# Expert layer: 224 tokens instead of 256 fetch their experts, in full 128-row gathers, and 288 instead of 256 meet all experts

## The chip, the cores and the metric

The kernel runs on one core of one Trainium2 chip. The metric is the device time of one execution in microseconds (us). A core has TensorE (PE; its weight loads are PEld), VectorE (DVE), ScalarE (ACT), GpSimd (POOL) and SyncE (SP), and 16 DMA engines that serve the queues of SP, ACT and POOL. MB are 10^6 bytes here, KB are 1024 bytes.

## The reference, cut to what matters

The program is two transformer blocks over 512 tokens of width 1024. The change is in the expert layer of the first block, where every token chooses 128 of 16384 experts (8 heads, 16 each) by two rounds of top-16 over products of keys:

```
s_top, i_top = lax.top_k(scores, PEER_TOPK)            # scores against 2 x 128 sub-keys per head
cand     = s_top[..., 0, :, None] + s_top[..., 1, None, :]
best, pos = lax.top_k(cand.reshape(..., 256), PEER_TOPK)
idx   = i_top[0] * 128 + i_top[1]   (at pos)           # 128 experts of each token
gates = jax.nn.softmax(best, axis=-1)
u = expert_u[it]; v = expert_v[it]                     # rows of 1024 fp32, 4 KB each
act = jax.nn.gelu(jnp.einsum("td,ted->te", xt, u), approximate=False)
return jnp.einsum("te,ted->td", gt * act, v)
```

## The kernel before

`peer()` computes this sum in two ways at once, for two halves of the tokens.

**The fetching tokens** (`NT = 256`, two tiles of 128 tokens, one token to a partition). For slot s of a tile, an indirect DMA from POOL (`fetch`, L1034) brings one expert row of 4 KB to each of the 128 partitions: 512 KB. `product` (L1005 in the profile, where the helper `dve` records everything) then multiplies it on DVE with the token's input row (`xt`) and sums it, for table `er`, or adds it with its gate to the output `y`, for table `ev`. That is 2 tiles x 128 slots x 2 tables = 512 gathers and 512 products. The rows lie in a ring of 8 in the buffers `xh` and `xl`; gathers are issued 6 products ahead (`LEAD`).

**The meeting tokens** (`ND = 256`) meet all 16384 experts in dense matmuls, 128 experts ("a row") at a time. In steps 0 to 127 of the loop `hidden(r)` multiplies 512 KB of weights of row r with the tokens `xb` (8 matmuls in fp32, which the trace shows as 16 records, L1078), and ACT applies the gelu a step later (L1085). In steps 128 to 255 `value(i)` multiplies row `order_v[i]` of the second table with gelu times gate (L1336), eight sums at once. The results of the gelu go to DRAM in pairs of rows (`ge_d`, L1089) and come back in the value steps (`ge`, L1301); the last `KEEP` = 16 rows stay. The gates stand in a grid `G` of 128 x 128 experts per token: `spread` builds it with one-hot matmuls, four tokens to a grid step (L1272 on PE; `sq` on DVE; `acc`, `gs` on ACT), writes it to DRAM 16 tokens at a time (L1278), and it is read back 16 rows at a time (L1316).

**The order.** The loop in `experts` writes the order of every engine by hand, step by step. `ROW` says how much DVE time by a planning rule a step takes (hidden rows without and with a grid step, value rows); `PACE` how far apart in such time two products stand, before and after the end of the top-16 work; `self.known` how many slots' indices exist. The top-16 work of `select` runs on DVE for tile 0, then for the two tiles of meeting tokens (2 and 3), then for tile 1: until that last one has made its `ix`, only the 128 slots of tile 0 can be gathered for table `er`, and the products stand one to a step or a little more. After it they stand about three to a step. In this text the **select stretch** goes from the first hidden matmul to the last reduction of `select`, the **gather stretch** from there to the landing of the last gather, and the **value stage** is the part of it with the value matmuls.

SP loads the weights in nine buffers in turn (`wraw`, `whi`, `wlo`, three each), so up to nine rows ahead of PE. Behind the loop the `y` tiles are transposed on PE (L1389) and added to `h`.

Of the kernel before, what the change touches and what calls it, by code (L numbers as in the profile page):

```python
# [18 lines left out]
T = 512  # L19
# [117 lines left out]
NT = 256  # L137
# [18 lines left out]
class Build:  # L156
# [809 lines left out]

    def peer(self):
        tc = self.tc
        with tc.tile_pool(name="pg", bufs=1) as pg:
# [12 lines left out]
            self.xt = pg.tile([128, 2, D], F32, name="xt")  # L982
# [44 lines left out]

    def fetch(self, upto):

        while self.nr < upto:  # L1030
            table, n = divmod(self.nr, 256)
            tt, s = divmod(n, 128)
            m = TOK[tt]
            self.nc.gpsimd.indirect_dma_start(  # L1034
                out=self.row(self.nr)[:m], out_offset=None,
                in_=self.A[("er", "ev")[table]].rearrange("j p a b -> (j p) (a b)"),
                in_offset=bass.IndirectOffsetOnAxis(ap=self.ix[:m, tt, s:s + 1], axis=0))
            self.nr += 1

    def product(self, pace):  # L1040

        n = self.nf
        if n >= self.known or self.spent < self.when + pace:
            return False
        self.when = self.spent
        self.fetch(n + 1)
        table, n = divmod(n, 256)
        tt, s = divmod(n, 128)
        m = TOK[tt]
        r = self.row(self.nf)[:m]  # L1050
        self.nf += 1
        if table == 0:
            self.dve("scalar_tensor_tensor", r, r, 1.0, self.xt[:m, tt], op0=OP.mult,
                     op1=OP.mult, accum_out=self.hid[:m, tt, s:s + 1])
        else:
            a, y = self.gate[:m, tt, s:s + 1], self.y[tt][:m]
# [6 lines left out]
        if table == 0 and s == 127:  # L1063
            h = self.hid[:m, tt]
            self.nc.scalar.activation(h, h, AF.Gelu)

            def weighted():
                self.dve("tensor_tensor", self.gate[:m, tt], self.gate[:m, tt], h, op=OP.mult)
            self.later(1, weighted)
        return True  # L1070
# [21 lines left out]
    def experts(self, pt, pw, pps):  # L1092
# [11 lines left out]
        self.gs2 = pw.tile([128, 2, 2048], F32, name="gs")  # L1104
        self.idx = pw.tile([128, 2, 5, 128], F32, name="idx")
# [35 lines left out]
        def select(tt, h0, n):  # L1141
# [88 lines left out]
            v("tensor_tensor", gt, gt, sm[:, :, None].to_broadcast([128, n, K]), op=OP.mult)  # L1230
            if TOK[tt] < 128:
                def turn():
                    tp = pps.tile([128, 4, 128], F32, name="gp", bufs=3)
                    idx = idx2[tt] = self.idx[:, tt % 2]
                    for i, t in enumerate((fin[:, 0], fin[:, 1], gt)):
                        te.transpose(tp[:, i], fl(t), self.ident)
                    s.activation(idx[:, :3], tp[:, :3], AF.Copy)
                    for i in range(2):
                        s.activation(idx[:, 3 + i], tp[:, 1 - i], AF.Copy, scale=-1.0)
# [3 lines left out]
        def spread(tt):  # L1243
# [6 lines left out]
            for tb in range((128 - TOK[tt]) // 16):  # L1250
                gs = gs2[:, tb % 2].rearrange("p (i t) -> p i t", t=16)
                for t4 in range(4):
                    o1 = self.nq.tile([128, 4, 128], F32, name="sq")
                    o2 = self.nq.tile([128, 4, 128], F32, name="acc")
                    i0 = TOK[tt] + tb * 16 + t4 * 4
# [30 lines left out]
        grids = (x for tt in (2, 3) for x in spread(tt))  # L1286
# [4 lines left out]
        order_v = [*range(119, 111, -1), *range(127, 119, -1), *range(111, -1, -1)]  # L1291
# [12 lines left out]
        def gates(i):  # L1304
# [3 lines left out]
            if i == 0:  # L1308
                self.gt2 = [pt.tile([128, NB * 256], F32, name="q")]
                self.y = [pt.tile([128, D], F32, name="kz"), pw.tile([128, D], F32, name="eq")]  # L1310
                self.a = pw.tile([128, 1280], F32, name="idx")
# [26 lines left out]
        with self.tc.manual_schedule(engines=ENGINES):  # L1338
            for r in range(5):
                load(r)  # L1340
            for tt in range(2):
                for half in range(2):
# [5 lines left out]
                    s.activation(self.xt[:m, tt, half * 512:(half + 1) * 512], tp[:m], AF.Copy)  # L1348
            end = 0.0
            while self.step < 256:  # L1350
# [15 lines left out]
                while self.spent < end:  # L1366
                    if self.product(PACE[work is None]):
                        continue
                    if work is None:
                        self.spent = end if self.nf == 512 else min(end, self.when + PACE[1])  # L1370
                    elif next(work, "end") == "end":
                        work = None
# [6 lines left out]
            assert not self.after  # L1379
        self.xh, self.xl = (self.cp.tile([128, 8, T], F32R, name=n) for n in ("xh", "xl"))  # L1380
        for d in range(8):
            h = self.h[:, d, NT:]
            v("tensor_tensor", h, h, yb[d][:, :ND], op=OP.add)
        for d in range(0, 8, 2):
            tp = self.pp.tile([128, T], F32, name="mm").rearrange("p (e t) -> p e t", e=2)
            for e in range(2):
                for tt in range(2):
                    m = TOK[tt]
# [634 lines left out]
```

## Time and profile before

| | before |
|---|---|
| median of 3 runs | 2758.99 us (2758.08 to 2763.65) |
| the profiled execution's own time | 2758.39 us |
| its span, first to last instruction | 2756.6 us |
| PE / PEld / DVE / ACT / POOL busy | 2442.9 / 2014.3 / 1831.3 / 932.0 / 1318.0 us |
| mean granted TensorE clock | 0.961 |
| DMA | 601.29 MB, mean 218 GB/s |

The busy times are sums over the whole program, in which stages with different limits follow each other. The expert layer's loop is the stretch from 615.6 us to 1833 us. A DMA share over 1 means that packets of the 16 engines overlap in the records.

### The profile page before, as it was taken

How to read it: one execution, taken by the hardware profiler on the slowest of the kernel's cores; microseconds unless marked ns; L12 is line 12 of the kernel's file. 1: busy time of each engine (PE TensorE's matmuls, PEld its weight loads, DVE VectorE, ACT ScalarE, POOL GpSimd, SP SyncE). 2: the span in 40 equal slices, each digit the busy share in tenths (PEclk: the TensorE clock that was granted, in tenths of full speed). 3: DMA queues.
4: the chain of work that ended last, by engine and by line, in shares of the span. 5: the costliest groups of instructions: out<-in, count | busy, mean ns of one | idle time of the engine just before them, and what ended most of it. 6: DMA issues, size and time to landing. Idle time of an engine off the chain costs nothing.

```text
span 2756.6 us, 33222 instructions
## 1 busy us (share of the span) xinstructions
PE 2442.9 (89%) x11548; PEld 2014.3 (73%) x11548; DVE 1831.3 (66%) x3674; ACT 932.0 (34%) x1806; POOL 1318.0 (48%) x930
## 2 busy tenths in 40 slices
PE   7999998999999999757777777888999998999997
PEld 5778877878889888646566666666777786777776
DVE  6655353367999997576676666785697758666226
ACT  4433243331148887000000000023477634333323
POOL 5433357343333235366566555654324555545543
PEclk9999999999999999979999899999999999999998
DMA  5311123139999999999999999952202352222332
GB/s 194 102 59 31 47 80 123 47 126 336 350 338 346 344 346 413 413 406 410 409 409 408 408 409 408 407 206 66 77 24 74 95 161 88 85 92 85 105 115 86
DMA packets 195368, 601.29 MB, mean 218 GB/s; under 512 B 23808, under 2 KB 44928, under 8 KB 193792
## 3 DMA queue, kind: packets, MB, share of 16 engines
q1 hardware_dynamic: 101664, 299.28, 31.1%
q0 software_dynamic: 73728, 268.47, 25.1%
q10 hardware_dynamic: 19808, 31.42, 3.2%
q8 instruction: 92, 1.51, 0.2%
q14 instruction: 76, 0.62, 0.1%
HBM read 556.62 MB, written 42.47 MB: 217 GB/s over the span
## 4 chain that ended last, share of the span: by engine, by line
PE 31%; DVE 27%; DMA 23%; issue 8%; ACT 6%; POOL 5%; ACTq 0%; DVEq 0%; POOLq 0%; SPq 0%
DMA xl<-in_ev_dram,ix 8%; DMA xl<-in_er_dram,ix 8%; DMA xh<-in_ev_dram,ix 7%; PE mm L227 7%; PE mm L228 6%; PE mm L226 6%; DVE y L1907 5%; PE mm L1078 3%; DVE xl L1005 2%; ACT whi L219 2%; DVE xh L1005 2%; PE dl L740 2%; DVE sq L1005 1%; POOL xh L1034 1%; POOL wlo L222 1%
## 5 line engine op out<-in xcount | busy, mean ns | idle before, releaser
L222 POOL TENSOR_TENSOR wlo<-wraw,whi 128x1024 fp32r<-128x1024 f32 (+5 forms) x212 | 466.0, 2203 | 463.0 <-ACT whi L219 458.2
L219 ACT ACTIVATE whi<-wraw 128x1024 fp32r<-128x1024 f32 (+4 forms) x213 | 204.3, 965 | 780.2 <-DMA wraw<-in_w_in_dram 517.5
L228 PE MATMUL mm<-xh,wlo 128*128 128x512 f32 (+1 forms) x1016 | 407.6, 402 | 18.6 <-POOL wlo L222 18.6
L227 PE MATMUL mm<-xl,whi 128*128 128x512 f32 (+1 forms) x1016 | 407.2, 401 | 5.9 <-DVE xl L341 3.1
L226 PE MATMUL mm<-xh,whi 128*128 128x512 f32 (+1 forms) x1016 | 402.9, 400 | 7.8 <-ACT xh L338 3.7
L1034 POOL DMA_INDIRECT xh<-in_er_dram,ix x128 | 149.6, 1169 | 214.2 <-DVE xh L1005 78.4
L228 PEld LDWEIGHTS mm<-xh,wlo 128*128 128x128 f32 (+1 forms) x1016 | 192.7, 190 | 65.8 <-POOL wlo L222 29.9
L227 PEld LDWEIGHTS mm<-xl,whi 128*128 128x128 f32 (+1 forms) x1016 | 192.9, 190 | 49.4 <-DVE xl L341 8.6
L1034 POOL DMA_INDIRECT xl<-in_er_dram,ix x128 | 137.2, 1072 | 191.1 <-DVE xl L1005 63.7
L226 PEld LDWEIGHTS mm<-xh,whi 128*128 128x128 f32 (+1 forms) x1016 | 192.7, 190 | 46.8 <-ACT xh L338 4.1
L1034 POOL DMA_INDIRECT xl<-in_ev_dram,ix x128 | 155.7, 1216 | 112.3 <-DVE eq L1005 38.5
L1034 POOL DMA_INDIRECT xh<-in_ev_dram,ix x128 | 151.4, 1183 | 100.9 <-DVE kz L1005 39.0
L1005 DVE SCALAR_TENSOR_TENSOR xh<-xh,xt 128x1024 f32<-128x1024 f32 x128 | 156.0, 1218 | 54.9 <-DMA xh<-in_er_dram,ix 54.5
L1907 DVE SCALAR_TENSOR_TENSOR y<-u,cvec,y 128x511 f32<-128x511 f32 (+1 forms) x88 | 137.3, 1563 | 74.3 <-ACT y L1905 72.8
L1005 DVE SCALAR_TENSOR_TENSOR xl<-xl,xt 128x1024 f32<-128x1024 f32 x128 | 155.9, 1218 | 41.7 <-DMA xl<-in_er_dram,ix 41.2
L1078 PE MATMUL mm<-xb,wlo 128*128 128x256 f32 x672 | 154.7, 384 | 8.7 <-DMA wlo<-in_eu_dram 8.7
L1078 PE MATMUL mm<-xb,whi 128*128 128x256 f32 x688 | 155.6, 379 | 2.6 <-DMA whi<-in_eu_dram 2.6
L1078 PE MATMUL mm<-xb,wraw 128*128 128x256 f32 x688 | 155.6, 379 | 0.0
L1078 PEld LDWEIGHTS mm<-xb,wlo 128*128 128x128 f32 x672 | 127.9, 193 | 26.5 <-issue 9.4
L1078 PEld LDWEIGHTS mm<-xb,whi 128*128 128x128 f32 x688 | 129.1, 190 | 19.6 <-issue 3.0
L1078 PEld LDWEIGHTS mm<-xb,wraw 128*128 128x128 f32 x688 | 129.1, 190 | 16.7
L1085 ACT ACTIVATE ge<-mm 128x256 f32<-128x256 f32 x128 | 48.4, 378 | 230.3 <-PE mm L1078 229.6
(671 smaller groups left out, 5371.1 us busy)
## 6 DMA issues: line engine op xcount, KB each, us to landing
wraw<-in_w_in_dram SPq DMA_DIRECT2D x57, 512.0 KB, 3.5
wraw<-in_w_up_dram SPq DMA_DIRECT2D x44, 512.0 KB, 3.5
wraw<-in_eu_dram SPq DMA_DIRECT2D x43, 512.0 KB, 6.9
whi<-in_eu_dram SPq DMA_DIRECT2D x43, 512.0 KB, 6.9
wlo<-in_ev_dram SPq DMA_DIRECT2D x43, 512.0 KB, 7.0
wraw<-in_ev_dram SPq DMA_DIRECT2D x43, 512.0 KB, 7.2
wlo<-in_eu_dram SPq DMA_DIRECT2D x42, 512.0 KB, 7.0
whi<-in_ev_dram SPq DMA_DIRECT2D x42, 512.0 KB, 7.2
```

The source lines that it names most:

```text
L219: nc.scalar.activation(hi, src, AF.Copy)
L222: (eng_lo or nc.vector).tensor_tensor(lo, src, hi.bitcast(F32), op=OP.subtract)
L226: t.matmul(ps, wh, xh, start=first, stop=False)
L227: t.matmul(ps, wh, xl, start=False, stop=False)
L228: t.matmul(ps, wl, xh, start=False, stop=last)
L740: te.matmul(ps[:, h * 128:(h + 1) * 128], lhs(h), rhs(h), start=True, stop=True)
L1005: return getattr(self.nc.vector, name)(out, *a, **kw)
L1034: self.nc.gpsimd.indirect_dma_start(out=self.row(self.nr)[:m], out_offset=None, in_=self.A[("er", "ev")[table]].rearrange("j p a b -> (j p ...
L1078: nc.tensor.matmul(ps[:, :ND], w[:, k], self.xb[:, k], start=k == 0, stop=k == 7)
L1085: nc.scalar.activation(self.pair[:, r % 2], ps[:, :ND], AF.Gelu)
L1907: v.scalar_tensor_tensor(y[:, j:], u[:, :T - j], w(2 - j), y[:, j:], op0=OP.mult, op1=OP.add)
```

## The change

`NT` becomes 224 and `ND` 288. Tile 0 keeps 128 tokens. Tile 1 has 96 tokens; its slots 96 to 127 are spread over the partitions 96 to 127, which serve tokens 0 to 31 of the tile in slots 0 to 31, tokens 32 to 63 in slots 32 to 63, and tokens 64 to 95 in slots 64 to 95. So tile 1 needs 96 gathers for each table, of 128 rows each: 448 gathers and products in all. For that, `ix` and `gate` of tile 1 are patched by three small DMAs each from ACT, `xt` by three DMAs (two at the start, one after slot 31), and the part of `y` on the last 32 partitions is put aside in `ys` after slots 31 and 63. The transposes behind the loop become plain matmuls with the identity or a selecting matrix, four instead of two per 128 columns.

The dense side gets 288 columns: matmuls of 288 instead of 256, `ge` pairs of 288 KB, a `G` with 18 instead of 16 blocks of tokens, 72 instead of 64 grid steps. `KEEP` falls from 16 to 6, so 61 instead of 56 pairs go through DRAM. `ROW` and `PACE` get new numbers, with a third pace of 2.2 for the products in the value steps.

```diff
-NT = 256
+NT = 224
 ND = T - NT
 NB = ND // 16
-KEEP = 16
-PACE = (2.6, 1.4)
-ROW = (4.0, 4.65, 3.85)
+KEEP = 6
+PACE = (2.6, 1.4, 2.2)
+ROW = (4.15, 5.05, 3.95)
+SLOTS = 128 + 96
...
             self.nc.gpsimd.indirect_dma_start(
-                out=self.row(self.nr)[:m], out_offset=None,
+                out=self.row(self.nr), out_offset=None,
...
-            self.dve("scalar_tensor_tensor", r, r, 1.0, self.xt[:m, tt], op0=OP.mult,
-                     op1=OP.mult, accum_out=self.hid[:m, tt, s:s + 1])
+            c = tt and 1 + s // 32 % 2
+            self.dve("scalar_tensor_tensor", r, r, 1.0, self.xt[:, c], op0=OP.mult,
+                     op1=OP.mult, accum_out=self.hid[:, tt, s:s + 1])
+            if tt and s == 31:
+                self.nc.scalar.dma_start(self.xt[96:, 1], self.xt[64:96, 1])
...
+            if tt and s in (31, 63):
+                if s == 31:
+                    self.ys = self.pg.tile([128, 3, D], F32, name="xt")
+                    self.nc.gpsimd.memset(self.ys[:96, :2], 0.0)
+                self.dve("tensor_copy", self.ys[96:, s // 32], y[96:])
+                self.dve("memset", y[96:], 0.0)
...
-                v("tensor_copy", self.ix[:, tt, sl], fl(far))
-                self.known = 128 * tt + (h0 + n) * K if tt == 0 else 512
+                m = TOK[tt]
+                v("tensor_copy", self.ix[:m, tt, sl], fl(far)[:m])
+                if tt:
+                    for k in range(3):
+                        p = slice(32 * k, 32 * k + 32)
+                        nc.scalar.dma_start(self.ix[96:, 1, p], self.ix[p, 1, 96:])
+                self.known = 2 * SLOTS if tt else (h0 + n) * K
...
+            if tt == 1:
+                s.activation(self.gate[:96, 1], fl(gt)[:96], AF.Copy)
+                for k in range(3):
+                    p = slice(32 * k, 32 * k + 32)
+                    nc.scalar.dma_start(self.gate[96:, 1, p], self.gate[p, 1, 96:])
...
-        grids = (x for tt in (2, 3) for x in spread(tt))
+        grids = (x for tt in (2, 3, 1) for x in spread(tt))
...
-                    if self.product(PACE[work is None]):
+                    if self.product(PACE[2 if i >= 0 else work is None]):
...
-                    te.transpose(tp[:, e, tt * 128:tt * 128 + m],
-                                 self.y[tt][:m, (d + e) * 128:(d + e + 1) * 128],
-                                 self.ident[:m, :m])
+                te.matmul(tp[:, e, :128], self.y[0][:, c], self.ident, start=e == 0, stop=False,
+                          skip_group_check=True)
+                te.matmul(tp[:, e, 128:NT], self.y[1][:, c], sel, start=False, stop=False,
+                          skip_group_check=True)
+                for k in range(2):
+                    o = 128 + 32 * k
+                    te.matmul(tp[:, e, o:o + 32], self.ys[:, k, c], self.ident[:, 96:],
+                              start=False, stop=k == 1, skip_group_check=True)
```

Where the end of the top-16 work falls can be read on ACT. The store `ge_d_43NN` is that of the hidden rows 2NN and 2NN+1, and the load of the exponential's table (L1225 before, L1244 after) stands at the end of tile 1's `select`. Before:

```order
L1085 ACTIVATE ge<-mm 128x256
L1089 DMA ge_d_4346<-ge 128x512
...
L1085 ACTIVATE ge<-mm 128x256
L1275 ACTIVATE gs<-gp 128x4x128
L1257 ACTIVATE acc<-row,idx 128x128 x4
L1258 ACTIVATE acc<-acc 128x512
L1225 ACT_TABLE_LOAD
L1225 ACTIVATE gate<-gate 128x128
```

and after the change, with the six small DMAs that patch `ix` and `gate`:

```order
L1098 ACTIVATE ge<-mm 128x288
L1102 DMA ge_d_4343<-ge 128x576
...
L1098 ACTIVATE ge<-mm 128x288
...
L1236 DMA ix<-ix 32x32 x3
L1244 ACT_TABLE_LOAD
L1244 ACTIVATE gt__7768<-gt__7768 128x128
L1251 ACTIVATE gate<-gt__7768 96x128
L1254 DMA gate<-gate 32x32 x3
```

The end of the top-16 work moved six hidden rows forward, from behind the gelu of row 94 to behind that of row 88. On DVE, 115 products (the rows that write `hid`) stand ahead of tile 1's cast to `ix` in both orders, and 148 rows `sq<-row,idx` before, 132 after.

In the value steps, DVE's order shows how many products (`kz<-xl,gate,kz`) stand to a value row (`idx<-ge,gs`, which makes the row's right-hand side). Before:

```order
L1005 TENSOR_TENSOR idx<-ge,gs 128x256
L1005 SCALAR_TENSOR_TENSOR kz<-xl,gate,kz 128x1024
L1005 SCALAR_TENSOR_TENSOR kz<-xh,gate,kz 128x1024
L1005 SCALAR_TENSOR_TENSOR kz<-xl,gate,kz 128x1024
L1005 TENSOR_TENSOR idx<-ge,gs 128x256
L1005 SCALAR_TENSOR_TENSOR kz<-xh,gate,kz 128x1024
L1005 SCALAR_TENSOR_TENSOR kz<-xl,gate,kz 128x1024
L1005 TENSOR_TENSOR idx<-ge,gs 128x256
```

and after:

```order
L1008 TENSOR_TENSOR idx<-ge,gs 128x288
L1008 SCALAR_TENSOR_TENSOR kz<-xh,gate,kz 128x1024
L1008 SCALAR_TENSOR_TENSOR kz<-xl,gate,kz 128x1024
L1008 TENSOR_TENSOR idx<-ge,gs 128x288
L1008 SCALAR_TENSOR_TENSOR kz<-xh,gate,kz 128x1024
L1008 TENSOR_TENSOR idx<-ge,gs 128x288
```

Before, two or three products stand to a value row, after it one or two. Over all, 205 products of 512 stand ahead of the first value row's turn in the loop before, and 230 of 448 after.

## Rows read from the trace of the kernel before

**Rows 1.** The span in 40 equal slices: DMA share, GB/s.

```profile
DMA  5311123139999999999999999952202352222332
GB/s 194 102 59 31 47 80 123 47 126 336 350 338 346 344 346 413 413 406 410 409 409 408 408 409 408 407 206 66 77 24 74 95 161 88 85 92 85 105 115 86
```

**Rows 2.** Stretches: length, busy (x instructions), granted clock, DMA share, GB/s.

```profile
615.60:1019.70 404.10, 389.33 (x1985) 345.71 (x1984) 368.22 (x1195) 213.35 (x504) 134.02 (x122) 1.00 0.96 342
1019.70:1196.50 176.80, 131.35 (x643) 113.09 (x641) 116.40 (x223) 67.67 (x162) 82.15 (x82) 0.90 1.02 405
1196.50:1833.10 636.60, 501.12 (x2049) 407.47 (x2050) 445.48 (x509) 3.21 (x4) 385.79 (x313) 0.93 1.01 400
1019.70:1821.20 801.50, 621.41 (x2641) 511.21 (x2640) 554.59 (x720) 69.04 (x164) 461.87 (x391) 0.92 1.02 405
```

**Rows 3.** The chain that ended last: start, length, what, around 1020 us.

```profile
1017.42 2.20 DVE fin L1005
...
1029.04 10.26 DMA xl<-in_er_dram,ix
```

**Rows 4.** Gathers (L1034) in the two stretches: POOL busy, clock, DMA share, GB/s.

```profile
615.60:1019.70 404.10, 134.02 (x122) 1.00 0.96 342
1019.70:1821.20 801.50, 459.92 (x390) 0.92 1.02 405
```

**Rows 5.** DMA issues, whole span: count, KB each, median us to landing.

```profile
G<-gs SPq DMA_DIRECT2D x16, 1024.0 KB, 10.8
...
ge<-ge_d SPq DMA_DIRECT2D x56, 256.0 KB, 7.5
...
q<-G SPq DMA_DIRECT2D x4, 2048.0 KB, 11.4
```

**Rows 6.** DMA issues from 615.6 to 1019.7 us.

```profile
ge_d<-ge ACTq DMA_DIRECT2D x47, 256.0 KB, 6.6
G<-gs SPq DMA_DIRECT2D x11, 1024.0 KB, 9.7
```

**Rows 7.** PE in order of time: start, length; hidden rows without, then with grid steps.

```profile
674.90 3.62 PE L1078 MATMUL mm<-xb,wraw 128*128 128x256 f32 x16
678.36 3.62 PE L1078 MATMUL mm<-xb,whi 128*128 128x256 f32 x16
...
866.83 1.05 PE L1272 MATMUL gp<-acc,sq 128*128 128x128 f32 x8
867.72 2.54 PE L1078 MATMUL mm<-xb,wlo 128*128 128x256 f32 x11
```

**Rows 8.** L1078 in the select stretch: PE and PEld busy (x records), clock, DMA.

```profile
615.60:1019.70 404.10, 340.96 (x1537) 288.62 (x1538) 1.00 0.96 342
```

**Rows 9.** L1272 in the select stretch, the same columns.

```profile
615.60:1019.70 404.10, 50.45 (x384) 50.42 (x384) 1.00 0.96 342
```

**Rows 10.** Waits from 1300 to 1800 us: us in total, times, longest.

```profile
PEld sp L1336 <- DVE idx L1005: 140.6, 71, 7.4
...
DVE kz L1005 <- DMA xh<-in_ev_dram,ix: 41.0, 43, 4.4
```

**Rows 11.** PE in order of time, at value row 49, behind a load of G.

```profile
1440.51 1.35 PEld L1336 LDWEIGHTS sp<-idx,wraw 128*128 128x128 f32 x4 [7.18 <-DVE idx L1005]
...
1442.38 2.34 PE L1336 MATMUL gp<-idx,wraw 128*128 128x256 f32 x6
```

**Rows 12.** Behind the loop, in order of time: the transposes and the sums after them.

```profile
1833.09 0.27 PE L1389 MATMUL mm<-ident,kz 128*128 128x128 f32 x1
...
1834.86 0.27 PE L1389 MATMUL mm<-ident,eq 128*128 128x128 f32 x1
...
1839.68 1.47 POOL L307 TENSOR_TENSOR acc<-acc,sq 128x512 f32<-128x512 f32 x1 [0.83 <-ACT sq L303]
...
1841.98 1.47 POOL L307 TENSOR_TENSOR acc<-acc,sq 128x512 f32<-128x512 f32 x1 [0.83 <-ACT sq L303]
```

**Rows 13.** Products on DVE, gather stretch: busy, mean ns; idle before.

```profile
L1005 DVE SCALAR_TENSOR_TENSOR kz<-xh,gate,kz 128x1024 f32<-128x1024 f32 x63 | 81.0, 1285 | 41.1 <-DMA xh<-in_ev_dram,ix 40.0
```

More of the change, by code (lines that the diff above doesn't have):

```diff
@@ L981, in peer @@
             self.xb = pg.tile([128, 8, ND], F32, name="xb")
-            self.xt = pg.tile([128, 2, D], F32, name="xt")
+            self.xt = pg.tile([128, 3, D], F32, name="xt")
             self.ix = pg.tile([128, 2, 128], U32, name="ix")
@@ L1046, in product @@
         self.fetch(n + 1)
[L1047 to L1050, printed above, removed]
+        table, tt, s = self.slot(n)
+        r = self.row(n)
         self.nf += 1
         if table == 0:
-            self.dve("scalar_tensor_tensor", r, r, 1.0, self.xt[:m, tt], op0=OP.mult,
-                     op1=OP.mult, accum_out=self.hid[:m, tt, s:s + 1])
+            c = tt and 1 + s // 32 % 2
[3 more added lines that the diff above has]
+                self.nc.scalar.dma_start(self.xt[96:, 1], self.xt[64:96, 1])
         else:
-            a, y = self.gate[:m, tt, s:s + 1], self.y[tt][:m]
+            a, y = self.gate[:, tt, s:s + 1], self.y[tt]
             if s == 0:
@@ L1060, in product @@
                 self.dve("scalar_tensor_tensor", y, r, a, y, op0=OP.mult, op1=OP.add)
+            if tt and s in (31, 63):
[4 more added lines that the diff above has]
+                self.dve("memset", y[96:], 0.0)
         self.spent += 0.08
         self.fetch(min(self.nf + LEAD, self.known))
-        if table == 0 and s == 127:
-            h = self.hid[:m, tt]
+        n = 96 if tt else 128
+        if table == 0 and s == n - 1:
+            h, g = self.hid[:, tt, :n], self.gate[:, tt, :n]
             self.nc.scalar.activation(h, h, AF.Gelu)
-            def weighted():
-                self.dve("tensor_tensor", self.gate[:m, tt], self.gate[:m, tt], h, op=OP.mult)
-            self.later(1, weighted)
+            self.later(1, lambda: self.dve("tensor_tensor", g, g, h, op=OP.mult))
         return True
@@ L1103, in experts @@
                allow_small_or_imprecise_dtypes=True)
-        self.gs2 = pw.tile([128, 2, 2048], F32, name="gs")
-        self.idx = pw.tile([128, 2, 5, 128], F32, name="idx")
+        self.gs2 = pw.tile([128, 2, NB * 128], F32, name="gs")[:, :, :2048]
+        self.idx = pw.tile([128, 5 * ND], F32, name="idx")
         qq = pt.tile([128, 2, NB * 128], F32, name="q")
@@ L1310, in gates @@
                 self.y = [pt.tile([128, D], F32, name="kz"), pw.tile([128, D], F32, name="eq")]
-                self.a = pw.tile([128, 1280], F32, name="idx")
+                self.a = pw.tile([128, 5 * ND], F32, name="idx")
             elif i == 16:
@@ L1347, in experts @@
                                      xa[:, 4 * half + i, tt * 128:tt * 128 + m], self.ident)
-                    s.activation(self.xt[:m, tt, half * 512:(half + 1) * 512], tp[:m], AF.Copy)
+                    c = slice(half * 512, (half + 1) * 512)
+                    s.activation(self.xt[:m, tt, c], tp[:m], AF.Copy)
+                    if tt:
+                        s.activation(self.xt[:m, 2, c], tp[:m], AF.Copy)
+            for k in range(2):
+                nc.scalar.dma_start(self.xt[96:, 1 + k], self.xt[32 * k:32 * k + 32, 1])
             end = 0.0
@@ L1366, in experts @@
                 while self.spent < end:
-                    if self.product(PACE[work is None]):
+                    if self.product(PACE[2 if i >= 0 else work is None]):
                         continue
                     if work is None:
-                        self.spent = end if self.nf == 512 else min(end, self.when + PACE[1])
+                        self.spent = end if self.nf == 2 * SLOTS else min(end, self.when + PACE[1 + (i >= 0)])
                     elif next(work, "end") == "end":
@@ L1379, in experts @@
             assert not self.after
+        sel = self.nq.tile([128, T], F32, name="sq")[:, :96]
+        v("tensor_copy", sel, self.ident[:, :96])
+        v("tensor_copy", sel[96:, 64:], self.ident[96:, 96:])
         self.xh, self.xl = (self.cp.tile([128, 8, T], F32R, name=n) for n in ("xh", "xl"))
```

27 lines of the change are left out of this document (16 added, 11 removed).

## The prediction

> **What bounds the kernel now.** I read the slices first, then cut the expert layer into stretches. From the tenth slice to the 26th the DMA engines are busy in nine tenths or more [rows 1], so the layer, not the rest of the program, is where a change of transfers counts; the rest (0 to 615 us, and from 1833 us on) is untouched and stays. Inside the layer there are two regimes. In the select stretch (615.6 to 1019.7 us) PE is busy for 389.3 of 404.1 us, DVE for 368.2, and the DMAs move 342 GB/s [rows 2]. The chain that ended last runs through DVE's top-16 work up to the last reduction at 1017.42 + 2.20 = 1019.6 us, and from 1029 us on through a landing gather [rows 3]. In the gather stretch behind it (1019.7 to 1821.2 us) the DMA share is 1.02 at 405 GB/s, while PE is busy for 621 and DVE for 555 of 801.5 us [rows 2]; PE waits for DVE's right-hand sides, and DVE for gathers [rows 10]. So the select stretch is set by PE and DVE, the gather stretch by bytes: 801.5 x 0.405 = 324.6 MB.
>
> At this point a rule speaks. The Trainium skill (DMA: Bandwidth & Descriptors, section "Where 436 GB/s comes from") lets a core's transfers from HBM to SBUF run at about 358 GB/s; the 405 of the row stand above it, so the trace disagrees and I go by the row. By the page's rate the 19.3 MB saved below would be worth 54 us instead of 48.
>
> **The select stretch: +7 us.** 115 products and the same top-16 work stand ahead of its end in both orders, but only 90 instead of 96 hidden rows (the ACT rows of the section on the change), so the change doesn't make the choice wait for six more rows of PE. A hidden row is 16 records and starts 3.46 us after the last, 216 ns a record [rows 7]. A record of 128 columns costs 0.89 / 8 = 111 ns with the change of line in it [rows 7]. Between the two a column costs 0.82 ns, so one of 288 columns costs 216 + 26 = 242 ns; scaled in proportion it would be 243. A row becomes 3.88 us. PE's work in the stretch: before 1537 records, so 96 rows x 3.46 = 332 [rows 8], and 384 records of grids, 48 steps x 0.89 = 43 [rows 9]; after 90 x 3.88 = 349 and 44 x 0.89 = 39. That is 13 us more. PE had 404.1 - 389.3 = 15 us free [rows 2], and DVE has 16 of its `sq` less. If the slack takes it all the cost is 0, if every present gap stays it is 13; I take the half, +7, since PE and DVE are both near their limit there and each waits now and then for the other. The select stretch ends at about 1026.7 us.
>
> **The gather stretch: 48 us less.** Its bytes, before and after, with the sizes of [rows 5]:
> - Gathers of 128 x 4 KB = 0.524 MB: 122 are issued ahead of it and 390 in it [rows 4]. After, 115 products and 6 or 7 in advance again make 122, so 448 - 122 = 326 are left: 64 x 0.524 = 33.6 MB less.
> - Weights of 0.524 MB a row: six hidden rows more fall into it, +3.1 MB.
> - Stores of `ge`: 56 - 47 = 9 pairs of 256 KB [rows 5, 6], 2.4 MB. After, the 61 pairs less the 44 of the first 88 rows, 17 of 288 KB, 5.0 MB: +2.7. Loads of `ge`: 56 x 0.262 = 14.7 to 61 x 0.295 = 18.0, +3.3.
> - Writes of G: 16 - 11 = 5 of 1 MB [rows 5, 6]; after, 18 less the 10 complete and written by grid step 44, 8: +3.1. Reads: eight of 2048 KB, 16.8 MB, to eight of 2304 KB, 18.9: +2.1.
>
> Sum: -33.6 + 3.1 + 2.7 + 3.3 + 3.1 + 2.1 = -19.3 MB. So 305.3 MB instead of 324.6, and at 405 GB/s 754 us instead of 801.5, -47.7. The three patches of `xt` add 0.4 MB, 1 us. The patches of `ix` and `gate` carry 4 KB each. ACT issues them where it waits for DVE anyway (the exponential of the same tile); the next gather of tile 1 is six products behind, and its index has until then to land. If that cover is gone, POOL's queue stands until they land, and behind it DVE's next products: once, 4 to 10 us like the landings of [rows 5].
>
> PE has room: 38 hidden rows, 128 value rows and 28 grid steps are 166 x 3.88 + 28 x 0.89 = 669 us of the 754. But it has less than it had. In the value stage a row took 636.6 / 128 = 4.97 us against 3.46 of work [rows 2, 7]; after, 1.7 gathers stand to a row instead of 2.5, so a row needs 0.89 + 0.52 + 0.15 + 0.15 = 1.71 MB, 4.2 us, against 3.88. When PE falls behind, SP's nine buffers fill, DVE can't run on past the five `a` slots, the ring of gathers fills, and the DMA engines stand. I charge 6 us for such moments; the bounds are 0 (the DMA share has no hole now) and 25 (the loads of G now cost PE up to 7 us each [rows 11]; half of that, eight times, would be 28, and the smaller demand of gathers takes some off).
>
> **The rest.** DVE's copies and memsets of `ys` are four operations on 1024 elements, at most 4 x 1.29 us by the products [rows 13], in a stretch in which DVE is idle for 247 us; POOL's memset likewise. They hide as long as DVE waits for gathers; uncovered they cost 5 us. Behind the loop PE does 32 matmuls of two records, each with its own weight load, instead of 16 of one record. Before, 16 took 1834.86 - 1833.09 + 0.11 = 1.9 us [rows 12]; 64 records at 111 ns are 7.1. The sums behind follow at 2.3 us for each of eight blocks [rows 12], so only the first pair shows: a quarter of 5.2, +1.3, between 0 and 5.
>
> **Sum.** 7 - 47.7 + 1 + 6 + 1.3 = -32.4. The profiled execution took 2758.4 us, the median of the runs is 0.6 above it: 2759.0 - 32.4 = **2727 us**.
>
> **Rivals.**
> *TensorE binds in the value stage, and the kernel is slower.* Of the gather stretch 176.8 x 0.405 = 71.6 MB lay ahead of the value stage; with 23 more gathers, six rows of weights and the stores above it is about 92.6 MB, 229 us, so the value stage starts at 1256 us instead of 1196.5. Its 128 rows are 497 us at full clock. The granted clock there is now 0.93 [rows 2]: behind a wait of 7.18 us six records take 2.34 us, against 1.3 us at 216 ns, so near the lower level of 1.2 GHz [rows 11]. At 0.93 the rows take 534 us, and if the eight loads of G still stop PE for 7 us each, 590: the end comes at 1846 instead of 1833 us, and with the tail the time is 2773. It decides when a row takes more than 577 / 128 = 4.5 us. The Trainium skill (TensorE: Matmul & The Clock Gate, section "HAM oscillation") says that a TensorE that waits for DMA between pieces starts each of them at half clock; the trace agrees with its row at 0.93. Against it: those waits come from the gathers, of which a row has a third less, and PE's share of the stage rises from 0.7 to over 0.9.
> *The writes slow the DMA engines.* In the select stretch they show a share of 0.96 at only 342 GB/s [rows 2], with G and `ge` being written. If the 92.6 MB ahead of the value stage go at that rate, they take 271 us instead of 229: +42, 2769 us. It decides below 92.6 / 261 = 0.355 MB/us. Against it: from 1019.7 to 1196.5 us the same writes go on and the rate is 405.
> *The change doesn't shorten the queue.* If the gathers in the value stage are hidden by PE anyway, the time stays at 2759. Against it stands the share of 1.02 [rows 2].
> *Everything hides.* No charge for select stretch and coupling: 2759.0 - 45.4 = 2714 us, a little less if DVE alone sets the select stretch.
>
> **Chances.** My forecast (2716 to 2742) 0.60. Everything hides (below 2716) 0.12. TensorE binds in the value stage, wholly or in part, 0.15: of that 0.05 still faster, 0.03 even, 0.07 slower. Slow writes 0.09: 0.02 even, 0.07 slower. No shorter queue 0.04, even. Within 0.2% (5.5 us) is what a measurement of this kernel can't tell from no change. So faster 0.77, same 0.09, slower 0.14. The range goes from 2704 (DVE alone sets the select stretch, a slightly better rate) up to 2758, which takes in the upper bounds of the charges (select +6, coupling +19, tail +4 make 2756) and the mild end of the first rival, and leaves out about 0.18. The forecast's own range is 2716 to 2742.
>
> **What would show it.** Right: the last `fin` of tile 1 ends between 1019 and 1034 us; hidden rows 3.88 us apart; 390 gathers behind it become about 326; a DMA share of about 1.0 and over 395 GB/s up to the last gather, which lands at about 1788 us; value rows of 4.1 to 4.4 us, with a higher granted clock than 0.93. Wrong: a share under 0.95 in the value stage with PE busy nearly throughout (the first rival), a rate of about 345 GB/s ahead of it (the second), a `fin` later than 1040 us (the select stretch goes by rows of PE after all), or a POOL queue that stands behind the patches of `ix`.

## The result, and the profile after

The changed kernel takes 2714.64 us (median of 4 runs, 2713.24 to 2716.18), the kernel before 2760.55 on the same chip (2758.08 to 2763.65): ratio 0.9832, 95% interval 0.982 to 0.9844, so 46 us or 1.7% faster. 2727 was forecast, with 2704 to 2758 for the range. The number lies below the forecast's own range (2716 to 2742) and on the fourth rival, "everything hides" (2714). The profiled execution took 2716.04 us with a span of 2714.3, 42.3 us below the 2756.6 of before. Line numbers moved: the hidden matmul L1078 is now L1091, the gather L1034 is L1041, the value matmul L1336 is L1362, the grid matmul L1272 is L1298, DVE's helper L1005 is L1008.

The 40 slices of the changed kernel, against [rows 1]:

```profile
DMA  5311123139999999999999999932102342222332
GB/s 192 106 63 32 39 74 125 62 113 322 338 334 336 335 344 367 411 415 409 410 409 409 409 409 409 406 106 75 58 22 80 122 146 78 86 89 88 102 118 85
```

The same stretches as [rows 2], with the first 37.4 us behind the selection apart (length, busy time of PE, PEld, DVE, ACT and POOL, granted clock, DMA share, GB/s):

```profile
612.70:1012.60 399.90, 398.71 (x1833) 320.81 (x1832) 365.14 (x1183) 195.30 (x453) 133.14 (x122) 1.00 0.96 337
1012.60:1050.00 37.40, 32.65 (x151) 26.20 (x150) 26.50 (x62) 28.14 (x69) 20.66 (x16) 0.91 0.86 309
1012.60:1246.70 234.10, 189.69 (x861) 150.60 (x859) 155.17 (x311) 118.40 (x281) 124.95 (x108) 0.92 1.00 396
1246.70:1780.20 533.50, 513.21 (x2048) 394.35 (x2049) 343.60 (x367) 3.30 (x6) 230.37 (x222) 0.98 1.01 401
1012.60:1772.50 759.90, 695.20 (x2876) 538.93 (x2875) 491.50 (x667) 120.64 (x286) 352.31 (x328) 0.96 1.02 403
```

The gathers alone in the select and the gather stretch (POOL busy, clock, DMA share, GB/s), against [rows 4]:

```profile
612.70:1012.60 399.90, 133.14 (x122) 1.00 0.96 337
1012.60:1772.50 759.90, 347.39 (x326) 0.96 1.02 403
```

Waits of the changed kernel from 1300 to 1800 us (total, times, longest), against [rows 10]:

```profile
DVE kz L1008 <- DMA xh<-in_ev_dram,ix: 51.8, 47, 5.5
...
PEld sp L1362 <- DVE idx L1008: 28.2, 21, 5.0
```

The gather stretch is 759.9 us long in place of 801.5 (-41.6), with 326 gathers in place of 390, at nearly the same rate and share. The value stage went from 636.6 to 533.5 us, and PE is now busy for 513 of them: from 1300 to 1800 us it waits 28 us for DVE's right-hand sides where it waited 141. The DMA engines at a share of 1.01 and PE at 0.96 stand close to each other there, so the profile alone doesn't say which of them sets the time.

The rest of the difference: the select stretch starts 2.9 us earlier and is 4.2 us shorter; the last value matmul ends 7.7 us behind the last landing (before 11.9); and from there to the end of the span it takes 934.1 us in place of 923.5, which gives 10.6 us back. -7.1 - 41.6 - 4.2 + 10.6 = -42.3. The 2.9 us come about in the program ahead of the layer, which the diff doesn't touch, and they say nothing about the change: e_patch and e_mend (below), whose instructions stand in the same order on every engine, enter the layer 4.1 us apart (612.6 and 616.7 us).

### The profile page after: what moved, and what is told of

The parts are those of the page before. It is cut to its first block, busy times and chain, and to the rows that moved or that the text cites. A ratio compares the mean times of both kernels' runs of the same rounds, so it can differ in the third digit from the quotient of the medians.

```text
span 2714.3 us, 33330 instructions
## 1 busy us (share of the span) xinstructions
PE 2529.4 (93%) x11663; PEld 2019.1 (74%) x11663; DVE 1772.2 (65%) x3608; ACT 965.5 (36%) x1876; POOL 1207.5 (44%) x867
## 4 chain that ended last, share of the span: by engine, by line
PE 46%; DMA 22%; DVE 18%; ACT 6%; issue 5%; POOL 3%; ACTq 0%; DVEq 0%; POOLq 0%; SPq 0%
PE mm L1091 12%; DMA xh<-in_ev_dram,ix 8%; PE mm L229 7%; PE mm L228 7%; DMA xl<-in_ev_dram,ix 7%; PE mm L227 6%; DVE y L1946 5%; DMA xh<-in_er_dram,ix 4%; ACT whi L220 2%; PE dl L741 2%; DMA xl<-in_er_dram,ix 2%; PE gp L1298 1%; PE mm L1362 1%; PE gp L1362 1%; POOL wlo L223 1%
## 5 line engine op out<-in xcount | busy, mean ns | idle before, releaser
L229 PE MATMUL mm<-xh,wlo 128*128 128x512 f32 (+1 forms) x1016 | 408.5, 402 | 18.7 <-POOL wlo L223 18.7
L1041 POOL DMA_INDIRECT xh<-in_er_dram,ix x112 | 126.4, 1128 | 192.6 <-DVE xh L1008 59.6
L1041 POOL DMA_INDIRECT xl<-in_er_dram,ix x112 | 126.8, 1132 | 185.0 <-DVE xl L1008 57.7
L1041 POOL DMA_INDIRECT xh<-in_ev_dram,ix x112 | 112.1, 1001 | 158.3 <-DVE kz L1008 82.2
L1041 POOL DMA_INDIRECT xl<-in_ev_dram,ix x112 | 115.2, 1029 | 145.9 <-DVE kz L1008 71.0
L1091 PE MATMUL mm<-xb,wraw 128*128 128x288 f32 x688 | 178.9, 414 | 0.0
L1091 PE MATMUL mm<-xb,whi 128*128 128x288 f32 x688 | 173.9, 406 | 0.0
L1091 PE MATMUL mm<-xb,wlo 128*128 128x288 f32 x672 | 172.4, 410 | 0.0
L1008 DVE SCALAR_TENSOR_TENSOR xh<-xh,xt 128x1024 f32<-128x1024 f32 x112 | 136.1, 1215 | 39.1 <-DMA xh<-in_er_dram,ix 39.0
L1008 DVE SCALAR_TENSOR_TENSOR xl<-xl,xt 128x1024 f32<-128x1024 f32 x112 | 136.2, 1216 | 37.8 <-DMA xl<-in_er_dram,ix 37.5
L1091 PEld LDWEIGHTS mm<-xb,wraw 128*128 128x128 f32 x688 | 132.2, 195 | 35.3
L1091 PEld LDWEIGHTS mm<-xb,whi 128*128 128x128 f32 x688 | 129.2, 190 | 33.6
L1091 PEld LDWEIGHTS mm<-xb,wlo 128*128 128x128 f32 x672 | 127.6, 193 | 33.3
L1098 ACT ACTIVATE ge<-mm 128x288 f32<-128x288 f32 x128 | 51.9, 407 | 234.5 <-PE mm L1091 221.6
```

Source lines behind the costliest of these rows:

```text
L229: t.matmul(ps, wl, xh, start=False, stop=last)
L1008: return getattr(self.nc.vector, name)(out, *a, **kw)
L1041: self.nc.gpsimd.indirect_dma_start(out=self.row(self.nr), out_offset=None, in_=self.A[("er", "ev")[table]].rearrange("j p a b -> (j p) (a ...
L1091: nc.tensor.matmul(ps[:, :ND], w[:, k], self.xb[:, k], start=k == 0, stop=k == 7)
L1098: nc.scalar.activation(self.pair[:, r % 2], ps[:, :ND], AF.Gelu)
```

## The experiments

All are edits of the changed kernel. "Theory A" is the prediction's: the gather stretch takes the time that its bytes take.

**TensorE's share and the bytes' share.** First e_pe, narrower value matmuls:

```diff
-                te.matmul(yb[d][:, :ND], w[:, d], a, start=i == 0, stop=i == 127)
+                te.matmul(yb[d][:, :256], w[:, d], a[:, :256], start=i == 0, stop=i == 127)
...
```

> The value matmuls run on 256 of their 288 columns; the value sums of the last 32 tokens are left out. Nothing else changes: the same weights, gathers and gate products. Theory A (bytes of the DMA set the value stage): 2711 to 2717 us, no change, and PE only waits more. Theory B (TensorE sets it, one row after another): a row falls from 3.88 us to the 3.46 of a 256-column row, 128 x 0.42 = 54 us, so about 2661 us. Theory C (the two take turns, a late gather once, a late matmul once): something between, 2685 to 2705 us.

Measured: 2721.78 us (2716.34 to 2723.98), ratio to before 0.9858 (0.9841 to 0.9874). Its value stage, then those of e_skip and e_skip_pe below:

```profile
1250.20:1783.10 532.90, 472.06 (x2048) 395.99 (x2048) 342.19 (x360) 4.09 (x7) 232.70 (x223) 0.96 1.01 402
```

```profile
1249.50:1753.20 503.70, 500.13 (x2048) 390.44 (x2049) 339.12 (x367) 3.30 (x6) 215.88 (x194) 0.99 1.00 396
```

```profile
1250.00:1744.40 494.40, 461.17 (x2048) 393.17 (x2049) 338.71 (x367) 2.24 (x5) 225.08 (x193) 0.97 1.01 402
```

PE's busy time fell by 41 us and the stage stayed at 532.9: B falls, and C, which wanted 2685 to 2705 us, falls with it. (The total lies 7 us above the changed kernel's, outside A's 2711 to 2717 too. In the profiled execution the layer starts 3.3 us later and the part behind the value stage takes 3.6 us more; neither is in the stage.) Then e_skip takes bytes away, in whole gathers, and e_skip_pe does both:

```diff
-            self.nc.gpsimd.indirect_dma_start(
...
+            if not (table and s % 8 == 7):
+                self.nc.gpsimd.indirect_dma_start(
...
```

> Every eighth gather of the value table is not issued (28 of 224, whole gathers of 128 rows); the product of such a slot takes what its buffer held. 28 x 524,288 bytes = 14.7 MB less, as many bytes as the gathers of 112 rows left out, but the other gathers keep all 128 partitions. Theory A (bytes at the rate of whole gathers, 409 GB/s): 36 us less than the changed kernel, 2675 to 2684 us. Theory B (TensorE): no change, 2709 to 2717 us. Theory C (the two take turns): 2685 to 2705 us.

> Every eighth value gather left out and the value matmuls on 256 of 288 columns. Theory A (bytes): as with the gathers alone, 2675 to 2684 us, and if the value stage there had come down to TensorE's own 497 us, up to 8 us less here. Theory B (TensorE): 54 us less than the changed kernel, 2661 us. Theory C: 2650 to 2675 us.

Measured: 2685.64 us (2683.89 to 2687.34) and 2679.24 (2675.8 to 2682.4). 29 of the 36 us came with the bytes alone, 35 with both. In e_skip PE is busy for 500.1 of 503.7 us: TensorE has become the bound, and the narrower matmuls, worth nothing before, are now worth 6 us of time and 9 of the stage. So in the changed kernel bytes set the value stage, and TensorE stands 30 us behind them. (By its number alone e_skip lies just above A's 2675 to 2684 us, at the edge of C's range; it is e_pe that rules C out. And e_skip takes whole gathers, so it does not tell their bytes from their number; the runs below, which take bytes and keep the number, change the rate as well.)

**Bytes taken away in smaller gathers.** Here the expectation broke. e_bytes takes the same 14.7 MB away as 16 rows of every value gather, e_both adds the narrower matmuls:

```diff
-                out=self.row(self.nr), out_offset=None,
+                out=self.row(self.nr)[:112 if table else 128], out_offset=None,
...
```

> The gathers of the value table fetch 112 of their 128 rows, and the sums over the last 16 partitions are taken of what the buffers held before; the number of gathers, products and matmuls stays. 224 x 16 x 4096 bytes = 14.7 MB less, at 403 bytes per ns. Theory A (bytes): 36 us less, about 2678 us, and the value stage falls to the 497 us of 128 rows of 3.88 us. Theory B (TensorE): no change, at most 5 us less, 2709 to 2717 us. Theory C (they take turns): 2685 to 2705 us.

> Both cuts together: value matmuls on 256 columns and value gathers of 112 rows. Theory A (bytes): as with the smaller gathers alone, about 2678 us. Theory B (TensorE): as with the narrower matmuls alone, about 2661 us. Theory C (they take turns): less than either alone, 2650 to 2675 us.

Measured: 2917.66 us (2911.55 to 2928.71) and 2912.41 (2908.16 to 2918.06), 200 us slower with fewer bytes; none of A, B and C says that. And e_half, which keeps the split at 224 but lets the second tile fetch with its own 96 partitions (its diff undoes the patches, `ys` and the 32 matmuls, sets the last pace to 1.6 in place of 2.2, and holds besides):

```diff
-SLOTS = 128 + 96
+SLOTS = 128 + 128
...
-                out=self.row(self.nr), out_offset=None,
+                out=self.row(self.nr)[:TOK[tt]], out_offset=None,
...
```

> The split at 224 tokens stays, but the second tile fetches with its own 96 partitions, 128 slots a table: 512 gathers in place of 448, with the same bytes; no patches of indices, gates and tokens, the sums turned by 16 transposes as before the change; the planner's last pace 1.6 in place of 2.2. Theory A (bytes): the same queue, less what sharing adds around it (about 6 us of thin DMA at the patches near 1016 us and about 5 us behind the loop), so 2702 to 2712 us. Rival D (the number of fetches and products counts): 64 more products of 1.28 us are 82 us of VectorE, of which the half in the value stage delays gates and value rows, so 2725 to 2755 us.

Measured: 2921.74 us (2914.68 to 2929.24). It is slower, as D has it, but far beyond D's 2725 to 2755 us, and its trace shows something else. e_half's DMA rate in its own 40 slices from 1500 to 1700 us; the second tile's value gathers begin at the 24th:

```profile
DMA  9999999999999999999999999999999999999999
GB/s 408 410 445 392 405 410 406 410 408 408 406 407 409 406 407 410 409 403 449 392 407 407 410 266 232 262 251 277 275 278 277 257 270 260 273 283 289 290 299 328
```

Within one 5-us slice, in one kernel, the rate falls from 410 to 266 GB/s while the share of busy time stays full. In stretches of e_half (the second tile's gathers of `er`, the first tile's of `ev`, the second's of `ev`):

```profile
1030.00:1160.00 130.00, 108.89 (x514) 88.22 (x513) 92.85 (x190) 74.11 (x180) 68.47 (x63) 0.92 1.04 319
...
1330.00:1600.00 270.00, 225.78 (x849) 166.85 (x848) 176.87 (x184) 0.31 (x1) 135.23 (x124) 0.94 1.03 404
1620.00:1950.00 330.00, 241.09 (x834) 173.53 (x832) 173.07 (x174) 0.00 (x0) 110.73 (x121) 0.89 1.04 267
```

And e_bytes from 1500 to 1700 us, by queue (packets, MB, share of 16 engines), behind the same rows of the changed kernel:

```profile
q0 software_dynamic: 11756, 42.80, 53.7%
q1 hardware_dynamic: 10614, 38.87, 48.8%
```

```profile
q0 software_dynamic: 7701, 27.61, 51.6%
q1 hardware_dynamic: 7698, 27.74, 51.6%
```

For the same busy time both queues carry two thirds: the gathers 27.6 MB for 42.8, and also the plain loads of weights, which the edit doesn't touch. So it isn't a cost of each gather, it is a slower rate of everything that moves beside gathers of 112 or 96 rows. Theory S, formed here: the rate goes by how many rows a gather has. e_dummy tests it by fetching 32 rows that nobody needs:

```diff
 (e_half)
...
-                out=self.row(self.nr)[:TOK[tt]], out_offset=None,
+                out=self.row(self.nr), out_offset=None,
...
```

> The kernel with the share undone (512 gathers, the second tile on its own 96 partitions), but its gathers fetch all 128 rows; the last 32 rows of each are of tokens that this half doesn't need and nobody reads them. 256 gathers x 32 x 4096 bytes = 33.5 MB more. Theory S (the chip moves a gather of 128 rows at 409 GB/s and one of 96 at 267 to 306, whatever it carries): 33.5 MB / 0.409 = 82 us over the changed kernel, less at most 6 us that sharing costs around it: 2790 to 2800 us, so over 120 us faster than the 2921.7 of the gathers of 96 rows that carry less. Rival N (512 gathers and 512 products in place of 448 are what made that kernel slow): 2920 us or more, since more bytes come on top.

Measured: 2799.79 us (2799.1 to 2802.9). 33.5 MB more and 122 us less: S holds and N falls. Both kernels have the same instructions in the same order on every engine; only the rows of the second tile's gathers differ. That tile's gathers of `er` and of `ev` in e_dummy:

```profile
1030.00:1160.00 130.00, 115.24 (x543) 92.39 (x542) 95.57 (x196) 82.08 (x195) 76.88 (x66) 0.95 1.03 410
...
1620.00:1830.00 210.00, 178.00 (x685) 131.58 (x684) 142.15 (x144) 0.00 (x0) 112.69 (x100) 0.97 1.03 408
```

The 82 us that 33.5 MB take at 0.409 MB/us are nearly all of the 85 us that e_dummy lies above the changed kernel; little is left for its 64 products more and its pace of 1.6. The last test, e_64, halves the value gathers:

> The value gathers fetch 64 of their 128 rows (the other half of the sums is taken of what the buffers held); 58.7 MB less in the value stage. If only counts that do not halve evenly are slow (64 rows at 409 GB/s): the queue would need 155 MB / 0.409 = 380 us, TensorE's 497 us bind, 2672 to 2685 us. If every gather of fewer than 128 rows is slow (276 GB/s or less, as 112 and 96 rows were): 155 / 0.276 = 562 us in place of 533, 2735 to 2750 us, and 2830 us at 200 GB/s.

Measured: 2773.24 us (2770.99 to 2775.26), 59 us above the changed kernel and above the 2735 to 2750 expected for 276 GB/s, though 58.7 MB fewer; 264 GB/s over its value stage:

```profile
1248.70:1836.90 588.20, 515.20 (x2048) 397.66 (x2049) 337.27 (x367) 2.24 (x5) 272.26 (x221) 0.94 1.01 264
```

So half of the rows isn't better than seven eighths of them: of 128, 112, 96 and 64 rows only 128 went at over 400 GB/s.

The Trainium skill (DMA: Bandwidth & Descriptors, section "The descriptor swizzle") says that in a transfer over 128 partitions each DMA engine writes to one port of SBUF. No run here shows ports, so whether smaller counts lose this, and why fewer rows go slower at all, stays open.

**The planner's numbers.** e_plan:

```diff
-PACE = (2.6, 1.4, 2.2)
-ROW = (4.15, 5.05, 3.95)
+PACE = (2.6, 1.4, 1.4)
+ROW = (4.0, 4.65, 3.85)
```

> The planner's numbers of before (rows of 4.0, 4.65 and 3.85 us, paces of 2.6, 1.4 and 1.4) in the changed kernel; all else stays. Theory A (bytes set the gather stretch, VectorE the selection): the order of products changes and the time does not, 2711 to 2718 us. Rival V (the paces set when products and gates meet on VectorE): with 1.4 the products come early in the planned order, gates stand behind products whose gathers have not landed, and rows wait: 2722 to 2740 us.

Measured: 2785.46 us (2784.38 to 2791.18), ratio to before 1.0087 (1.0072 to 1.0103): 71 us slower than with the new numbers, and slower than before the change. Its select stretch up to the start of the last `fin`, the value stage while there are gathers, and the end of it:

```profile
617.80:1045.90 428.10, 424.51 (x1949) 341.27 (x1948) 367.50 (x1192) 212.43 (x492) 134.19 (x121) 1.00 0.93 325
1225.90:1750.00 524.10, 434.09 (x1604) 320.44 (x1605) 353.80 (x382) 0.28 (x1) 270.19 (x245) 0.93 1.03 408
1750.00:1858.50 108.50, 107.81 (x445) 84.20 (x444) 19.17 (x37) 2.90 (x3) 6.38 (x3) 1.00 0.49 163
```

The same bytes moved at the same rate, and the last gather was issued at 1743.9 us, 17 us earlier than in the changed kernel. But the products that fetch them had taken VectorE's turns, and PE had waited for right-hand sides: 82.2 us from 1300 to 1700, against 27.9 in the same stretch of the changed kernel:

```profile
PEld sp L1362 <- DVE idx L1008: 82.2, 42, 7.1
```

So some 28 value rows were left when the gathers were done, and ran for 108 us beside DMA engines that were half idle. V holds, and dearer than expected: the select stretch, too, is 30 us longer. (The row above ends where the last `fin` starts; up to its end at 1048.2 us it is 430.4 us, with PE busy for 426.8, in place of 399.9.) With fewer us planned to a hidden row the order puts the end of the choice behind six more rows (behind the gelu of row 94 in place of 88), and DVE now waits for PE there. DVE's waits for PE's grids from 612 to 1020 us, in e_plan and then in the changed kernel:

```profile
DVE sq L1008 <- PE gp L1298: 14.7, 18, 1.5
```

```profile
DVE sq L1008 <- PE gp L1298: 2.3, 4, 1.5
```

The two numbers were not tried apart.

**The hole at 1012 us.** e_patch issues the copies of `ix` and `gate` on SP's queue. e_mend was to issue the second tile's first gathers earlier as well:

```diff
-                        nc.scalar.dma_start(self.ix[96:, 1, p], self.ix[p, 1, 96:])
+                        nc.sync.dma_start(self.ix[96:, 1, p], self.ix[p, 1, 96:])
...
 (e_mend, behind self.known = ...)
+                if tt:
+                    self.fetch(min(self.nf + LEAD, self.known))
```

> The six copies that carry indices and gates to the last 32 partitions are issued from SP's queue in place of ScalarE's; no other difference. Theory P (ScalarE's 1.81 us of issues ahead of the exponential, with VectorE 5.15 us and POOL 6.93 us waiting behind, thin the DMA queue at 1012 to 1022 us for good): 3 to 5 us less than the changed kernel, 2709.5 to 2712 us, and 350 GB/s or more where it was 309 from 1012.6 to 1050 us. Rival Q (what was late there is made good behind it, since the value stage waits on gathers with slack of its own): 2713 to 2716 us. Rival R (SP's queue stands behind the copies, whose indices come late, and weights arrive late): 2716 to 2720 us.

> The copies of indices and gates from SP's queue, and the first six gathers of the second tile issued as soon as its indices are known, ahead of VectorE's wait for the exponential. Theory P (thin DMA at 1012 to 1050 us is time lost): with the copies alone 330 GB/s came there in place of 309 and 1.7 us less; with gathers 2 us earlier 345 to 375 GB/s and 2709 to 2712.5 us. Rival Q (made good behind it): 2712.5 to 2716 us.

Measured: 2712.95 us (2711.51 to 2715.92) and 2713.18 (2709.39 to 2715.76), neither to be told from the changed kernel; P's 2709.5 to 2712 us, and then 2709 to 2712.5, were not reached. e_mend turned out to be e_patch once more: six gathers are in advance at that point already, so its `fetch` issues nothing, and its instructions stand in the same order as e_patch's on every engine. What stands in the hole is seen in the changed kernel in order of time (start, length; in brackets the wait ahead):

```profile
1014.04 0.94 POOL L1041 DMA_INDIRECT xh<-in_er_dram,ix  x1 [2.40 <-DVE far L1008]
...
1016.16 1.81 ACTq L1236 DMA_DIRECT2D ix<-ix  x3
...
1019.64 0.29 DVE L1008 TENSOR_REDUCE sm<-gt__7768 128x8 f32<-128x128 f32 x1 [5.15 <-ACT gt__7768 L1244]
...
1020.54 0.18 PEld L1262 LDWEIGHTS gp<-ident,gt__7768 128*128 128x128 f32 x1 [4.98 <-DVE gt__7768 L1008]
...
1021.90 0.94 POOL L1041 DMA_INDIRECT xl<-in_er_dram,ix  x1 [6.93 <-DVE sq L1008]
```

and in e_patch:

```profile
1018.14 0.29 DVE L1008 TENSOR_REDUCE sm<-gt__7768 128x8 f32<-128x128 f32 x1 [3.66 <-ACT gt__7768 L1244]
...
1020.40 0.94 POOL L1041 DMA_INDIRECT xl<-in_er_dram,ix  x1 [5.44 <-DVE sq L1008]
```

A gather is issued when a product has been done, and DVE does no product while its sum over the gates waits for ACT's exponential. ACT has eight small steps of the grid, the three copies and a table to load ahead of it. PE stands for these gates too, 4.98 us, and from 1019.6 to 1023.4 us the DMA engines move 5 GB/s, at a share of 0.03. Without the copies the wait is 1.5 us shorter, the gather comes 1.5 us earlier, and the 37.4 us from 1012.6 move 330 GB/s in place of 309 (350 was expected): 0.8 MB, 1.9 us at 403. That fits the 1.7 us between the medians, which the runs can't tell from nothing. P has the mechanism, but the copies are the smaller part of the hole; the rest of the wait might go if products stood in between, as one product and four `sq` do in the kernel before (DVE waits for no exponential there). That was not tried.

**Behind the loop.** e_tail carries the sums of the first two thirds in the loop:

```diff
+                k = s // 32
+                self.nc.scalar.dma_start(self.ys[32 * k:32 * k + 32, 2], self.ys[96:, k])
+            if tt and s == 80:
+                self.dve("tensor_tensor", y[:64], y[:64], self.ys[:64, 2], op=OP.add)
...
-                for k in range(2):
-                    o = 128 + 32 * k
-                    te.matmul(tp[:, e, o:o + 32], self.ys[:, k, c], self.ident[:, 96:],
-                              start=False, stop=k == 1, skip_group_check=True)
```

> The sums that the last 32 partitions took for the first two thirds are carried in the loop, by two copies and one addition of 64 x 1024 on VectorE (about 1.3 us), into the rows that they belong to; behind the loop 16 matmuls of 128 columns turn them in place of 32. Theory T (the 16 extra matmuls and their wait are on the path behind the loop): 2 to 5 us less than the changed kernel, 2709.5 to 2712.5 us. Rival U (the additions of the sums to the token rows go with VectorE and the next stage, and the loss lies in a different order of the later stages): 2713 to 2716 us.

Measured: 2715.09 us (2714.73 to 2716.86), no difference. DVE's first and last sum of token rows behind the loop in the changed kernel, and ACT's step there, in order of time; then the same in e_tail:

```profile
1782.22 0.62 DVE L1008 TENSOR_TENSOR h<-h,mm 128x448 f32<-128x448 f32 x1 [1.25 <-PE mm L1429]
...
1783.26 0.79 ACT L220 ACTIVATE whi<-wraw 128x704 fp32r<-128x704 f32 x1 [7.18 <-DMA wraw<-in_w_kg_dram]
...
1787.58 0.62 DVE L1008 TENSOR_TENSOR h<-h,mm 128x448 f32<-128x448 f32 x1 [0.51 <-PE mm L1429]
```

```profile
1786.41 0.62 DVE L1008 TENSOR_TENSOR h<-h,mm 128x448 f32<-128x448 f32 x1 [0.41 <-PE mm L1428]
...
1789.17 0.55 DVE L1008 TENSOR_TENSOR h<-h,mm 128x448 f32<-128x448 f32 x1
1790.34 0.79 ACT L220 ACTIVATE whi<-wraw 128x704 fp32r<-128x704 f32 x1 [9.50 <-DMA wraw<-in_w_kg_dram]
```

The four sums now take 3.3 us from the first to the last, in place of 6.0. But ACT, which does the squares of the norm next, has the split of a weight ahead of them that lands only then, and starts the squares 5.7 us behind the end of the value stage in place of 3.8; so PE's first sum of squares comes 23.7 us behind the last value matmul, and 23.5 in the changed kernel. What the matmuls gave, that wait took. From the last value matmul to the end of the span it is then 928.0 us in e_tail and 934.1 in the changed kernel. But it is 935.3 in e_patch and 928.8 in e_mend, whose code behind the loop is the changed kernel's and whose instructions stand in the same order; so some 6 us there come and go from one execution to the next, for which I know no cause. (e_tail's value stage began 3.4 us later and took 1.7 more, which is why nothing of this shows in its time.) With the 16 transposes of before it is 923.5 (before), 924.7 (e_half) and 924.4 (e_dummy).

## Why the prediction came out as it did

The mechanism held, and 2727 was 12 us too high. In the profiled executions the start of the layer and the select stretch gave 14 us more than forecast, the end of the value stage 4 and the gather stretch 1, and the tail took 9 of that back; the rest lies between the profiled executions and the medians. The 2.9 us at the start of the layer and some 6 us of the tail come and go between executions of one order of instructions (e_patch and e_mend), so part of the number is chance.

- **The bound.** Right. The gather stretch goes by bytes: e_pe leaves the value stage as it is, e_skip takes 29 of 36 us.
- **The gather stretch's bytes, -47.7 us.** Right: 326 gathers as forecast, 759.9 x 0.403 = 306.2 MB against 305.3, 92.7 MB ahead of the value stage against 92.6 (234.1 x 0.396). This step had a condition that the prediction didn't see: a byte saved counts only if the other gathers keep 128 rows. The last 32 partitions' change of thirds is what keeps it; without it (e_half) the same bytes cost 207 us more, with an altered pace, which e_dummy has too.
- **Coupling, +6, and the patches of `xt`, +1.** With the bytes -40.7 was forecast, and -41.6 came. The coupling was another one than I named, though. The step "ACT issues them where it waits for DVE anyway" fails: ACT issues them ahead of the exponential for which DVE waits, and POOL stands 6.93 us behind DVE. The copies alone are 1.5 us of that (e_patch); the rest is DVE's wait for the exponential, with no product in between, for which the sum had no term. In the 37.4 us behind the selection 309 GB/s came, where before 377 had come at that place: 2.5 MB or 6 us, which is all of the charge. Little is left for PE that falls behind in the value stage, which the charge was made for. That the indices have six products' time to land held.
- **The select stretch, +7 us: wrong in sign.** It became 4.2 us shorter, and its last `fin` ended at 1012.6 us, ahead of the 1019 to 1034 that were to show the forecast right. The hidden rows are 3.88 us apart as worked out. The step that failed is "I take the half, +7, since PE and DVE are both near their limit": PE went to 398.7 busy of 399.9 us and took up all of its slack, and DVE waited for PE's grids for only 2.3 us, so the wider matmuls cost next to nothing. That the stretch fell below the lower bound of 0 goes with DVE's work, 365.1 us for 368.2: its 16 fewer `sq` were named and not priced. But no slack is left: the chain that ended last, of which PE's hidden rows were 9% from 700 to 1010 us before the change, has them at 75% after it, so which of the two engines sets the 399.9 us is not settled. e_plan shows how close it is: with the old numbers the end of the choice lies six rows later, DVE waits for PE, and the stretch is 430 us long.
- **The tail, +1.3 us: mis-sized.** It measured +10.6 from the last value matmul to the end. "Only the first pair shows" fails: the pairs' sums stand 1.78 us apart behind their matmuls, and the norm's first sum of squares on PE comes 4.8 us later behind the last value matmul than before (23.5 us for 18.7). That the matmuls are the cause is not shown, since e_tail takes 16 of them away and has 23.7, with ACT held by a weight. The other 5.8 us arise in later stages, whose code the diff doesn't touch, and are no more than what e_patch and e_mend differ by there.
- **The end of the value stage** was forecast 12 us behind the last landing, as before, and was 7.7.
- **The rivals.** TensorE binding: no (e_pe), though it comes 30 us behind the bytes, and the clock rose from 0.93 to 0.98. Slow writes: no, 396 GB/s ahead of the value stage and 413 from 1050 us on. "Everything hides" has the number, by errors that cancel: the select stretch gave 7 us and the value stage's end 4, which it did not count, and the tail took 10.6.
- **The planner's numbers** were read as part of the order, and that the kernel's gain hangs on them was no rival. With the old ones it is 25 us slower than before the change: a way to the other side, bigger than the two that were priced as slower (2773 and 2769 us).

## What to carry to other kernels

When a stretch goes by bytes, ask of each gather not only how many bytes it has but whether it keeps all 128 partitions: here 33.5 MB of padding made a kernel 122 us faster. When a change shifts the balance of two streams that take turns on one engine (gathers' products and PE's right-hand sides on VectorE), their pacing must be set again so that both end together; the change without its numbers lost 71 us. And a small issue is free only if nothing stands behind it on its engine that another engine waits for (here 1.5 us).

## What the runs showed of the hardware

Gathers of 4-KB rows beside plain loads moved 408 to 410 GB/s with 128 rows to a gather, 274 with 112 (over e_bytes's value stage), 267 (value table) and 319 (other table, with writes of G beside; 410 there with 128 rows) with 96, and 264 with 64, with the DMA engines busy throughout (a share of 1.01 or more). With 112 rows the plain loads slowed by the same factor as the gathers, for the same busy time. Three copies of 4 KB within SBUF took 4.0 to 4.4 us each from issue to landing, at a mean DMA share of 0.49 from the first issue to the last landing (1016.2 to 1021.8 us).
